# The second part of each weight block: negation on ScalarE and an adding transfer

## The chip, the cores and the metric

The kernel runs on one core of a Trainium2 chip. The metric is the device time of one execution in microseconds, the median of several runs. Inputs lie in HBM, and all weights are read from there once.

## The reference

The program computes two transformer-like blocks over 512 tokens of width 1024 in float32. What matters here is that nearly all its work is matrix products with weights. Cut down:

```
x = x + rmsnorm((sigmoid gates * [ssd_branch(z, xbc, dt), window_attention(q, k, v)]) @ w_o)
x = x + rmsnorm(square(relu(rmsnorm(x) @ w_mlp_in)) @ w_mlp_out)      # 1024 -> 4096 -> 1024
x = x + parallel_mixer(rmsnorm(x))       # mLSTM and latent attention, then w_out
x = x + memory_cross_attention(rmsnorm(x), rmsnorm(mem))
x = x + square(relu(rmsnorm(x) @ w_ff1)) @ w_ff2                      # 1024 -> 4096 -> 1024
```

`z`, `xbc`, `dt`, `q`, `k`, `v` and the gates are columns of one product `rmsnorm(x) @ w_in`. The two MLPs alone hold 64 of the 143 weight blocks described next.

## The kernel before, in words

A float32 product is made of three faster ones. A float32 number is split into a rounded part (type float32r, "hi") and the rest ("lo"), and `hi*xh + hi*xl + lo*xh` stands for `w*x`. So each weight block has to be split before TensorE can use it whole.

The weights come as a stream of 143 blocks, the class `Unit`. Most are 1 MB: 128 partitions, 8 k-tiles, 256 columns. Three tiles belong to a unit: `raw` (as loaded), `whi` and `wlo`, each with two buffers.

- `load()` (line 129) issues the transfer from HBM to `raw` on SyncE's queue (SP).
- `split()` works in two halves of 128 columns. For each half, ScalarE copies `raw` to `whi` with rounding (line 140), and VectorE subtracts, `wlo = raw - whi` (line 141).
- `use(key)` splits the unit if that hasn't been done, and calls `ahead`, which splits the next unit and starts the load of the one after it.

So a unit is split while TensorE works on the unit before it. Its `whi` and `wlo` slots come free when TensorE has read the unit before that one, and a `raw` slot comes free when the readers of the split are done with it.

TensorE's readers come in two kinds. `cm` (channel-major, lines 266 to 268) takes 128 columns of the unit at a time, so its first step needs one half of `wlo` only. `tm` (token-major, lines 284 to 286) takes 128 tokens and all columns, so its first step needs both halves. The woven product `cm4` (lines 1022 to 1024), the query product of the cross-attention (lines 1597 to 1599) and the mixer's projection (lines 1225) and latents read both halves early too.

In the MLPs, `f_evac` works on each 128 columns of the first product: ScalarE makes relu and its rounded square (`ua_h`, lines 1161 and 1162), GpSimd the square `fsq` (line 1164), VectorE the rest `ua_l` (line 1165). The second product is added up in `acc` on VectorE (line 1171). Elsewhere GpSimd adds squares for the norms (line 986), raises to powers (line 323), rotates (line 1279) and issues a few small transfers (lines 561, 626, 1383). A scheduler sets the order on each engine from the program's text. Within an engine the order is then fixed.

Of the kernel before, what the change touches and what calls it, by code (L numbers as in the profile page):

```python
# [43 lines left out]
# columns of w_in  # L44
Z0, XBC0, DT0, Q0, K0, V0, G0 = 0, 2048, 6144, 6208, 7232, 7488, 7744
# columns of w_in_2
U0, VM0, OP0, IF0 = 0, 512, 1024, 1536

# columns of the packed constants
# [3 lines left out]
def packed_constants():  # L53
    """Constants that depend on shapes alone: the identity and its mirror image, the rotary
    frequencies, the one-hot of the relative position buckets, and the fixed rows of the products
    that make the exponents of the decays."""
# [11 lines left out]
    # rows 0..7 choose the chunk, rows 64..127 the pair that a token is in  # L68
# [4 lines left out]
    # rows 8..15 choose the head, rows 64..127 hide the pairs of tokens that a direction doesn't see  # L73
# [11 lines left out]
def body(ctx, tc, a, out, dbg=None):  # L85
# [26 lines left out]
    # ---------------------------------------------------------------- weights, as a stream of blocks  # L112
    win, win2 = a["w_in"][0], a["w_in_2"][0]

    class Unit:
        """A block of weights [128, kt, n], split into two parts of float32r whose sum it is."""
# [14 lines left out]
        def split(self):  # L131
            if self.hi is None:
                self.load()
                self.hi = self.view(wp.tile([P, WN], F32R, name=nm("whi"), tag="whi", bufs=2))
                self.lo = self.view(wp.tile([P, WN], F32R, name=nm("wlo"), tag="wlo", bufs=2))
                n = self.flat or self.n
                for c in range(0, n, max(P, n // 2)):
                    e = min(n, c + max(P, n // 2))
                    sl = (slice(None), slice(c, e)) if self.flat else (slice(None), slice(None), slice(c, e))
                    A.copy(self.hi[sl], self.raw[sl])  # L140
                    V.tensor_tensor(out=self.lo[sl], in0=self.raw[sl], in1=self.hi[sl].bitcast(F32), op=ALU.subtract)  # L141
# [11 lines left out]
    def use(key, lag=False):  # L153
        """The unit; the next one is split at once or, with lag, where ahead() says."""
# [5 lines left out]
    def ahead(key, *behind):  # L160
        """The next unit being split, behind the given instructions, and the one after it on its way."""
# [9 lines left out]
    def evac_first(key, evac, *args):  # L171
        """evac, with the next unit's split behind the first of it on each engine."""
# [78 lines left out]
    # ---------------------------------------------------------------- helpers  # L251
    def cm(key, act, evac, parts=1):
        """Steps of a channel-major product: evac(j, psum) for each 128 columns of the unit, each in
        one step or more."""
# [19 lines left out]
    def tm(key, act, evac, ntile=NT):  # L274
        """Steps of a token-major product: evac(t, psum) for each 128 tokens."""
# [20 lines left out]
    def weave(main, side):  # L296
        """The steps of both lists, each list spread evenly."""
# [13 lines left out]
    def split_from(src, hi, lo, gain=None):  # L311
        """hi + lo = src * gain (a column of gains), both float32r."""
# [7 lines left out]
    def inv_rms(dst, ssq, n, width):  # L320
        """dst = (ssq / n + eps) ** -0.5 for [128, width] columns."""
# [3 lines left out]
    def token_sums(ssq, tag="t"):  # L325
        """Sums over the partitions of [128, 512], token-major in PSUM [128, 4]."""
# [5 lines left out]
    def bcast_tokens(r, tag="t"):  # L332
        """[128, 4] token-major -> PSUM [128, 512] on every partition."""
# [5 lines left out]
    # ---------------------------------------------------------------- persistent tiles  # L339
# [17 lines left out]
    # ---------------------------------------------------------------- block 1, first norm  # L357
# [12 lines left out]
    # the tensor engine's clock is at its full rate when the first inputs are here  # L370
# [34 lines left out]
    # ---------------------------------------------------------------- parameters, as columns  # L405
# [34 lines left out]
    # ---------------------------------------------------------------- dt and the decays  # L440
# [14 lines left out]
    # what the products for the exponents take: see ssd_exponents  # L455
# [4 lines left out]
    def dt_evac(_, po):  # L460
        """Rows (half, direction, head), two chunks of tokens in each half."""
# [17 lines left out]
        # cumulative sums of dt * a in each chunk, forwards and backwards  # L479
# [13 lines left out]
        # cs in two float32r parts, by way of DRAM, where the heads of a group are one row  # L493
# [8 lines left out]
        # the logarithm of dt, less cs, in two parts too  # L502
# [11 lines left out]
        # token-major: exp(cs) and dt * exp(tot - cs)  # L514
# [14 lines left out]
        def late():  # L529
# [8 lines left out]
            # the decay over a whole chunk, on every partition; step k takes chunk k and chunk 3 - k  # L538
# [25 lines left out]
    # ---------------------------------------------------------------- block 1, SSD branch  # L564
# [22 lines left out]
    class Group:  # L587
        """The SSD branch of one group of four heads."""
# [5 lines left out]
        # products, convolution and layouts  # L594
# [27 lines left out]
        # rows of the products for the exponents  # L622
# [32 lines left out]
        def exponents(self, c):  # L655
            """dt[s] exp(cs[l] - cs[s]) of both directions: cs[l] comes from rows 0..7,
            log(dt) - cs[s] from rows 8..15; rows 64..127 hide what overflows on the wrong side, and
            the select what is next to the diagonal."""
# [110 lines left out]
    # ---------------------------------------------------------------- block 1, window attention  # L769
# [8 lines left out]
    # the bias over relative positions, one row for each head, read back as a Hankel block: the  # L778
    # queries of each block are taken in reverse
# [18 lines left out]
    def keys(kv):  # L798
        """The two parts of the keys of a head, each on both halves of the partitions."""
# [11 lines left out]
    def q_steps(u, parts=1):  # L811
        """Queries of a head, in reverse in each block: one part on its own half of the partitions,
        the other part on the other half."""
# [12 lines left out]
    class Pair:  # L826
        """Heads 2 p and 2 p + 1, which have the same keys."""
# [59 lines left out]
        def turn(self, b):  # L887
            """The weights over their sum, transposed, with the queries in order again."""
# [71 lines left out]
    # ---------------------------------------------------------------- residual stream and norms  # L960
# [11 lines left out]
    class SumSq:  # L972
        """Sums of squares over the tiles of a channel-major array."""
# [19 lines left out]
    def post_norm(gain, ssq, next_gain, side):  # L993
        """xT += norm(acc) * gain, and the parts of xT * next_gain; returns the sums of squares of xT.
        The steps of another product run meanwhile."""
# [14 lines left out]
    def cm4(k1, k2, act, evac, lag=3):  # L1010
        """Two units, channel-major, with the parts of the activations taken as they come."""
# [23 lines left out]
    # ---------------------------------------------------------------- block 2, the memory  # L1035
# [25 lines left out]
    # rotary tables with the gains of the norms in them  # L1061
# [84 lines left out]
    def inv_ms_bcast(xsq):  # L1146
        """1 / (mean square + eps) of each token, on every partition."""
# [7 lines left out]
    def mlp(b, xsq, fin, side=(), last=None):  # L1155
        """The tiles of relu(h w1)^2 w2, h without its rms and rb the square of that: fin(m, psum, rb)
        gets the last quarter, the others being in acc, last(m, rb) is called before that."""
# [47 lines left out]
    # ---------------------------------------------------------------- block 2, parallel mixer  # L1205
# [8 lines left out]
    # gates, latents and the shared key: token-major  # L1214
# [42 lines left out]
    # both parts of a head's row are taken by one product  # L1257
# [15 lines left out]
    def rope(dst, src, tabs):  # L1273
        """dst = rotated src [128, 4, 64], the gains being in the tables."""
# [474 lines left out]
```

## Time and profile before

| | |
|---|---|
| median of 3 runs | 1943.59 us (1941.83 to 1944.87) |
| span of the profiled execution | 1939.5 us |
| TensorE (PE) busy | 1868.0 us, 96% |
| VectorE (DVE) busy | 1083.4 us, 56% |
| ScalarE (ACT) busy | 856.8 us, 44% |
| GpSimd (POOL) busy | 482.8 us, 25% |
| DMA, loads from SP (q1) | 157322 packets, 151.03 MB, 24.8% of 16 engines' time |
| DMA, issued by GpSimd (q0) | 2496 packets, 1.61 MB, 0.3% |

The span runs from the first to the last instruction; about 4 us of the measured time lie outside it. The busy table tells which engine has no time left. The windows tell the same for one stage. The timeline of one unit tells how long before its use a split is done, which the sums don't.

### The profile page before, as it was taken

The page shows a single profiled execution, that of the slowest core. Times are in us where ns is not written, and L with a number is a line of the kernel's source. Part 1 is how long each engine was busy: PE and PEld are TensorE (multiplying, and loading weights), DVE is VectorE, ACT ScalarE, POOL GpSimd, SP SyncE. Part 2 cuts the span into 40 slices and gives each one's busy share as a digit, 9 for nine tenths or more (in the row PEclk, how much of TensorE's full clock was granted, in tenths as well). Part 3 has the DMA queues.
Part 4 walks back from the last instruction along what each step waited for, and adds up shares of the span by engine and source line. Part 5 has one row for each costly group of instructions (what it writes and reads, how often), then busy time and mean ns, then how long its engine had stood idle before and what let it go on. Part 6 is the DMA issues. An engine that isn't in the chain of part 4 may idle for free. (4 is left out here: it accounts for less than half of the span.)

```text
span 1939.5 us, 24660 instructions
## 1 busy us (share of the span) xinstructions
PE 1868.0 (96%) x9685; PEld 1541.4 (79%) x9685; DVE 1083.4 (56%) x1751; ACT 856.8 (44%) x1397; POOL 482.8 (25%) x530
## 2 busy tenths in 40 slices
PE   8989999999999999998999999989999999999999
PEld 6878778887887777887888888888877778888887
DVE  7767773777555654537334334667567763334543
ACT  5655652755335665345332323444453543323231
POOL 1544450444202221233011202322110431111020
PEclk9999999999999999999999999999999999999999
DMA  6222122221222221333333332322111213232322
GB/s 174 68 67 67 45 67 87 67 67 44 82 94 82 82 78 66 119 122 109 98 109 98 101 94 89 114 73 74 51 45 65 87 44 108 90 107 87 109 87 65
DMA packets 169377, 164.10 MB, mean 85 GB/s; under 512 B 8742, under 2 KB 165101, under 8 KB 169262
## 3 DMA queue, kind: packets, MB, share of 16 engines
q1 hardware_dynamic: 157322, 151.03, 24.8%
q10 hardware_dynamic: 9444, 9.89, 1.6%
q0 software_dynamic: 2496, 1.61, 0.3%
q8 instruction: 76, 1.25, 0.3%
q14 instruction: 39, 0.32, 0.1%
HBM read 158.26 MB, written 4.23 MB: 84 GB/s over the span
## 5 line engine op out<-in xcount | busy, mean ns | idle before, releaser
L141 DVE TENSOR_TENSOR wlo<-raw,whi 128x1024 fp32r<-128x1024 f32 (+2 forms) x285 | 374.9, 1329 | 277.8 <-ACT whi L140 275.4
L140 ACT CAST whi<-raw 128x1024 fp32r<-128x1024 f32 (+2 forms) x285 | 288.3, 1029 | 408.9 <-PE psg L267 381.1
L266 PE MATMUL psg<-hh,whi 128*128 128x512 f32 (+1 forms) x1016 | 403.0, 397 | 0.8 <-DVE hl L318 0.8
L267 PE MATMUL psg<-hl,whi 128*128 128x512 f32 (+1 forms) x1016 | 400.7, 394 | 0.0
L268 PE MATMUL psg<-hh,wlo 128*128 128x512 f32 (+1 forms) x1016 | 399.3, 393 | 0.0
L266 PE MATMUL psg<-ua_h,whi 128*128 128x512 f32 x800 | 316.5, 396 | 0.5 <-DVE xT L1562 0.5
L267 PE MATMUL psg<-ua_l,whi 128*128 128x512 f32 x800 | 313.4, 392 | 0.0
L268 PE MATMUL psg<-ua_h,wlo 128*128 128x512 f32 x800 | 312.3, 390 | 0.0
L266 PEld LDWEIGHTS psg<-hh,whi 128*128 128x128 f32 (+1 forms) x1016 | 191.0, 188 | 40.5 <-issue 1.2
L268 PEld LDWEIGHTS psg<-hh,wlo 128*128 128x128 f32 (+1 forms) x1016 | 190.7, 188 | 39.7
L267 PEld LDWEIGHTS psg<-hl,whi 128*128 128x128 f32 (+1 forms) x1016 | 190.8, 188 | 38.1 <-DVE hl L315 0.4
L1164 POOL TENSOR_TENSOR fsq<-relu 128x512 f32<-128x512 f32 x64 | 80.9, 1264 | 507.9 <-ACT relu L1161 434.5
L266 PEld LDWEIGHTS psg<-ua_h,whi 128*128 128x128 f32 x800 | 150.1, 188 | 35.4 <-DVE xT L1562 2.4
L267 PEld LDWEIGHTS psg<-ua_l,whi 128*128 128x128 f32 x800 | 150.3, 188 | 32.3 <-DVE ua_l L1165 1.2
L268 PEld LDWEIGHTS psg<-ua_h,wlo 128*128 128x128 f32 x800 | 150.2, 188 | 30.7
L284 PE MATMUL psg<-whi,hh 128*128 128x256 f32 x416 | 121.5, 292 | 2.7 <-ACT sz L608 2.7
L286 PE MATMUL psg<-whi,hl 128*128 128x256 f32 x416 | 121.8, 293 | 0.0
L285 PE MATMUL psg<-wlo,hh 128*128 128x256 f32 x416 | 120.5, 290 | 1.0 <-DVE wlo L141 1.0
L986 POOL TENSOR_TENSOR ssq<-ssq,sq 128x512 f32<-128x512 f32 x42 | 66.4, 1582 | 117.0 <-ACT sq L985 116.0
L1165 DVE TENSOR_TENSOR ua_l<-fsq,ua_h 128x512 fp32r<-128x512 f32 x64 | 47.3, 739 | 79.2 <-POOL fsq L1164 79.2
L284 PEld LDWEIGHTS psg<-whi,hh 128*128 128x128 f32 x416 | 81.5, 196 | 5.9 <-ACT sz L608 4.0
L285 PEld LDWEIGHTS psg<-wlo,hh 128*128 128x128 f32 x416 | 81.4, 196 | 1.6 <-DVE wlo L141 1.2
(560 smaller groups left out, 2910.4 us busy)
## 6 DMA issues: line engine op xcount, KB each, us to landing
raw<-in_w_in_dram SPq DMA_DIRECT2D x37, 1024.0 KB
raw<-in_w_ff_dram SPq DMA_DIRECT2D x32, 1024.0 KB
raw<-in_w_mlp_in_dram SPq DMA_DIRECT2D x16, 1024.0 KB
raw<-in_w_mlp_out_dram SPq DMA_DIRECT2D x16, 1024.0 KB
raw<-in_w_in_dram SPq DMA_DIRECT2D x16, 512.0 KB
raw<-in_w_ssd_out_dram SPq DMA_DIRECT2D x8, 1024.0 KB
raw<-in_w_attn_out_dram SPq DMA_DIRECT2D x4, 1024.0 KB
raw<-in_w_o_dram SPq DMA_DIRECT2D x4, 1024.0 KB
```

The source lines that it names most:

```text
L140: A.copy(self.hi[sl], self.raw[sl])
L141: V.tensor_tensor(out=self.lo[sl], in0=self.raw[sl], in1=self.hi[sl].bitcast(F32), op=ALU.subtract)
L266: T.matmul(o, lhsT=u.hi[:, k, c:e], rhs=xh[k], start=k == 0, stop=False)
L267: T.matmul(o, lhsT=u.hi[:, k, c:e], rhs=xl[k], start=False, stop=False)
L268: T.matmul(o, lhsT=u.lo[:, k, c:e], rhs=xh[k], start=False, stop=k == u.kt - 1)
L284: T.matmul(o, lhsT=xh[k][:, tk], rhs=u.hi[:, k, 0 : u.n], start=k == 0, stop=False)
L285: T.matmul(o, lhsT=xh[k][:, tk], rhs=u.lo[:, k, 0 : u.n], start=False, stop=False)
L286: T.matmul(o, lhsT=xl[k][:, tk], rhs=u.hi[:, k, 0 : u.n], start=False, stop=k == u.kt - 1)
L986: G.tensor_tensor(out=self.t, in0=self.t, in1=q, op=ALU.add)
L1164: G.tensor_tensor(out=f, in0=r, in1=r, op=ALU.mult)
L1165: V.tensor_tensor(out=ua_l[:, m, :], in0=f, in1=ua_h[:, m, :].bitcast(F32), op=ALU.subtract)
```

## The change

For each half of a unit, the subtraction on VectorE goes. In its place ScalarE writes the negative of `raw` into `wlo`, and since `wlo` is of type float32r, what it writes is the negative of the rounded value. Then GpSimd issues a transfer from `raw` to `wlo` within SBUF that adds to what is there: `wlo = -hi + raw`. The rest of the diff removes comments and a docstring, and from line 142 on all lines of the new kernel are one further down.

```
                     A.copy(self.hi[sl], self.raw[sl])
-                    V.tensor_tensor(out=self.lo[sl], in0=self.raw[sl], in1=self.hi[sl].bitcast(F32), op=ALU.subtract)
+                    A.activation(self.lo[sl], self.raw[sl], AF.Copy, scale=-1.0)
+                    nc.gpsimd.dma_start(out=self.lo[sl], in_=self.raw[sl], accum_op=ALU.add)
```

The waits follow: the transfer waits for ScalarE's negation, a reader on TensorE waits for the transfer of its half (`tm` for both), and the next load into the same `raw` slot waits for both transfers. VectorE's list gets 285 instructions shorter, ScalarE's longer by 285 passes and ten table loads, GpSimd's by 285 transfers.

On ScalarE, in the first product of the first MLP (before):

```order
L1161 ACTIVATE relu_9306<-psg_9281 128x512
L1162 ACTIVATE ua_h<-relu_9306 128x512
L140 CAST whi_9343<-raw_9279 128x8x128
L1161 ACTIVATE relu_9337<-psg_9312 128x512
L140 CAST whi_9343<-raw_9279 128x8x128
L1162 ACTIVATE ua_h<-relu_9337 128x512
```

The same place after:

```order
L1162 ACTIVATE relu_9401<-psg_9376 128x512
L1163 ACTIVATE ua_h<-relu_9401 128x512
L140 CAST whi_9438<-raw_9374 128x8x128
L1162 ACTIVATE relu_9432<-psg_9407 128x512
L141 ACTIVATE wlo_9439<-raw_9374 128x8x128
L1163 ACTIVATE ua_h<-relu_9432 128x512
L140 CAST whi_9438<-raw_9374 128x8x128
L141 ACTIVATE wlo_9439<-raw_9374 128x8x128
```

The first negation stands behind the second relu, and the second copy now stands behind the rounded square.

On GpSimd, in the same product (before; `fsq` are the squares of two halves of a unit):

```order
L1164 TENSOR_TENSOR fsq_9239<-relu_9236 128x512
L1164 TENSOR_TENSOR fsq_9270<-relu_9267 128x512
L1164 TENSOR_TENSOR fsq_9309<-relu_9306 128x512
L1164 TENSOR_TENSOR fsq_9340<-relu_9337 128x512
L1164 TENSOR_TENSOR fsq_9379<-relu_9376 128x512
L1164 TENSOR_TENSOR fsq_9410<-relu_9407 128x512
```

The same place after:

```order
L142 DMA wlo_9305<-raw_9250 128x8x128 x2
L142 DMA wlo_9367<-raw_9312 128x8x128 x2
L1165 TENSOR_TENSOR fsq_9404<-relu_9401 128x512
L1165 TENSOR_TENSOR fsq_9435<-relu_9432 128x512
L142 DMA wlo_9439<-raw_9374 128x8x128 x2
L1165 TENSOR_TENSOR fsq_9476<-relu_9473 128x512
```

Both transfers of a unit stand behind two squares. The first two rows are units of the second product before it, where nothing stands between.

On GpSimd in the mixer (before; `lat` and `rs` are powers for norms, `ro` rotations):

```order
L323 TENSOR_TENSOR lat_10207<-lat_10207,mhalf 128x4 x3
L1279 TENSOR_TENSOR ro_10252<-pj_9955,tk_10203 128x128
L1279 TENSOR_TENSOR ro_10256<-pj_9955,tk_10203 128x128
L323 TENSOR_TENSOR rs_1620_10498<-rs_1620_10498,mhalf 128x4 x3
L1279 TENSOR_TENSOR ro_10518<-pj_10405,tq_10205 128x128
L1279 TENSOR_TENSOR ro_10522<-pj_10405,tq_10205 128x128
```

The same place after:

```order
L142 DMA wlo_10470<-raw_10147 128x8x128 x2
L142 DMA wlo_10481<-raw_10477 128x320 x2
L324 TENSOR_TENSOR lat_10392<-lat_10392,mhalf 128x4 x3
L1280 TENSOR_TENSOR ro_10437<-pj_10138,tk_10388 128x128
L1280 TENSOR_TENSOR ro_10441<-pj_10138,tk_10388 128x128
L142 DMA wlo_10621<-raw_10488 128x8x128 x2
L142 DMA wlo_10655<-raw_10628 128x8x128 x2
L324 TENSOR_TENSOR rs_1620_10691<-rs_1620_10691,mhalf 128x4 x3
```

Transfers of four units stand among the powers and rotations, which wait for results of the products.

## Rows read from the trace of the kernel before

**Rows 1.** Page, busy us (share of the span) and number of instructions of each engine:

```profile
PE 1868.0 (96%) x9685; PEld 1541.4 (79%) x9685; DVE 1083.4 (56%) x1751; ACT 856.8 (44%) x1397; POOL 482.8 (25%) x530
```

**Rows 2.** Groups by line and shape: busy us, mean ns | idle before, releasers:

```profile
L141 DVE TENSOR_TENSOR wlo<-raw,whi 128x1024 fp32r<-128x1024 f32 x275 | 368.6, 1354 | 274.5 <-ACT whi L140 274.3
...
L140 ACT CAST whi<-raw 128x1024 fp32r<-128x1024 f32 x275 | 283.6, 1048 | 408.5 <-PE psg L267 381.1 <-issue 11.4 <-PE pse L1226 9.6
...
L665 ACT ACT_TABLE_LOAD x25 | 32.1, 1283 | 0.4
...
L620 ACT ACTIVATE sz<-sz 128x1024 f32<-128x1024 f32 x8 | 8.5, 1060 | 0.0
```

**Rows 3.** First MLP by window: us, busy of PE to POOL, clock, DMA share, GB/s:

```profile
860.00:1205.00 345.00, 339.95 (x1550) 279.78 (x1549) 146.12 (x160) 121.56 (x171) 63.59 (x51) 1.00 0.32 101
```

**Rows 4.** Timeline, one unit of the first MLP: start us, duration us, instruction [idle before]:

```profile
1042.40 2.00 ACT L140 CAST whi<-raw 128x1024 fp32r<-128x1024 f32 x2 [6.24 <-PE psg L267]
...
1043.48 1.22 DVE L141 TENSOR_TENSOR wlo<-raw,whi 128x1024 fp32r<-128x1024 f32 x1 [0.21 <-ACT whi L140]
...
1044.62 1.22 DVE L141 TENSOR_TENSOR wlo<-raw,whi 128x1024 fp32r<-128x1024 f32 x1
...
1045.87 0.37 SPq L129 DMA_DIRECT2D raw<-in_w_mlp_in_dram  x1
...
1053.23 1.05 ACT L140 CAST whi<-raw 128x1024 fp32r<-128x1024 f32 x1 [8.83 <-PE psg L267]
...
1053.71 0.39 PE L268 MATMUL psg<-ua_h,wlo 128*128 128x512 f32 x1
```

**Rows 5.** DMA queue of loads, 132 to 143 us, then 1045.5 to 1056.3: packets, MB, share:

```profile
q1 hardware_dynamic: 2080, 1.05, 35.5%
...
q1 hardware_dynamic: 1040, 1.05, 33.1%
```

**Rows 6.** Small transfers issued by GpSimd: instruction ns min/median/max; after it its landing:

```profile
L626 POOL DMA_DIRECT2D rh<-csd x16: 507/552/641, 42.5 to 424.5; - x16
...
DMA to landing us min/median/max: 1.9/2.0/3.0
...
L1383 POOL DMA_DIRECT2D rows_h<-mk x4: 499/514/648, 1339.6 to 1341.2; - x4
...
DMA to landing us min/median/max: 1.7/1.7/1.9
...
L561 POOL DMA_DIRECT2D rh<-in_consts_dram x2: 540/666/792, 12.2 to 14.1; - x2
```

**Rows 7.** Timeline at the start: unit 1's first copy, and its first product with `wlo`:

```profile
17.77 1.09 ACT L140 CAST whi<-raw 128x1024 fp32r<-128x1024 f32 x1
...
20.75 0.40 PE L268 MATMUL psg<-hh,wlo 128*128 128x512 f32 x1
```

**Rows 8.** Copy and first use of `wlo`, first and last of five units, one half:

```profile
751.55 1.04 ACT L140 CAST whi<-raw 128x1024 fp32r<-128x1024 f32 x1
...
758.46 0.48 PE L268 MATMUL psg<-hh,wlo 128*128 128x512 f32 x1
...
1597.25 1.04 ACT L140 CAST whi<-raw 128x1024 fp32r<-128x1024 f32 x1
...
1603.07 0.39 PE L268 MATMUL psg<-hh,wlo 128*128 128x512 f32 x1
```

**Rows 9.** The same, first and last of eight units that read both halves:

```profile
865.78 1.05 ACT L140 CAST whi<-raw 128x1024 fp32r<-128x1024 f32 x1 [1.07 <-PE psg L267]
...
874.08 0.28 PE L285 MATMUL psg<-wlo,mm_h 128*128 128x256 f32 x1
...
1514.42 1.04 ACT L140 CAST whi<-raw 128x1024 fp32r<-128x1024 f32 x1
...
1519.95 0.39 PE L1599 MATMUL pse<-hh,wlo 128*128 128x512 f32 x1
```

**Rows 10.** Waits of PE: engine line waited for: us in total, times, longest us:

```profile
PE psc L634 <- ACT cT L573: 8.6, 6, 2.3
PE pst L712 <- DVE ua_l L318: 5.8, 4, 2.6
```

## The prediction

> **What bounds the kernel now.** I read four views, in this order. The first is the page's busy table: TensorE works for 1868.0 of 1939.5 us [rows 1], so 71.5 us are idle in all, and no edit that only frees other engines can gain more than a part of them. The second is the table of groups: the line that this change replaces, the subtraction on VectorE, costs 368.6 us of VectorE's time, and the rounding copy ahead of it 283.6 us of ScalarE's [rows 2]. Neither is on the path by its size. The third is the table by windows: in the first MLP TensorE works 339.95 of 345.00 us at a granted clock of 1.00, ScalarE 121.56, GpSimd 63.59, and the DMA engines are at 0.32 of their time [rows 3]. So the stage has room on every engine but TensorE. The fourth is the timeline of one weight unit there [rows 4]: rounding copies from 1042.40, the two subtractions from 1043.48 to 1045.84, the raw slot's next load issued at 1045.87, and the first product with this unit's second part at 1053.71, after a period of 10.83 us (1042.40 to 1053.23). Of 11.31 us from first copy to first use, the old path for the first half uses 2.30 (1.08 to the subtraction, 1.22 of it). That leaves 9.0 us of cover in an ordinary unit. What the change has to be asked is where the cover is thinner than the new path is long.
>
> **The cost of the new path.** Removed: 285 VectorE subtractions. Added: 285 ScalarE passes and 285 adding transfers issued by GpSimd. For one half unit of 128 x 1024:
>
> 1. The copy, 1.05 us [rows 2].
> 2. The negating pass. A ScalarE activation of this size from SBUF to SBUF has a row, 1.06 us [rows 2]. With 0.1 us of hand-over the chain is at 2.2.
> 3. The transfer's fixed part. GpSimd's small transfers land a median of 2.0 us after issue (32 rows) or 1.7 (4 rows), and the issuing instruction takes a median of 0.51, 0.55 and 0.67 us for 4, 32 and 128 rows [rows 6]. I put 2.0 and 0.3 for the step from ScalarE to the issue: 4.5.
> 4. The data. A half is 8 k-tiles of 128 columns in each of 128 partitions, so 1024 pieces of 512 bytes, 64 for each of 16 DMA engines. No row has an adding transfer. Nearest below: a plain load in pieces of 512 bytes, 35.5% of 11 us on 16 engines for 2080 packets, 30 ns a piece. Nearest above: the same engines with pieces of 1 KB, 33.1% of 10.8 us for 1040 packets, 55 ns [rows 5]. An adding piece reads two operands of 512 bytes and writes one, so 1 KB read is what I take it to be like: **55 ns**, 3.5 us for a half. The ends are 30 ns (the second read costs nothing) and 60 (it costs a whole plain piece more).
>
> So the first half is ready 8.0 us after its copy starts. The second half's negation is done at 4.3, its transfer queues behind the first, and both are ready at 11.5. At 30 ns it is 6.4 and 8.5, at 60 ns 8.3 and 12.2.
>
> **Where that is covered.** In a unit of the MLP's second product: 8.0 of 11.31 us. In the first product the order on ScalarE puts a relu (0.6 us) between copy and negation, and on GpSimd both squares ahead of the transfers, so that the first is issued about 3.2 us after the copy and lands at 9.0: still covered, by 2.3. The raw slot comes free at 11.5 instead of 3.4, its load starts 8 us later and has until the second unit from now, 21.7 us after the copy. The DMA engines per period of 10.83 us: 3.57 for the load (33.1% of 10.8) and 2 x 3.5 for the additions, 10.6 in all. That fits, by 2%. The same goes for units of the other stages with periods of 11 to 20 us. I charge nothing there, and a few nanoseconds more a piece would make this the bound (rival B).
>
> **Where it isn't.** I took the time from first copy to first use of the second part for all 143 units. Outside of these it is 9.0 us or more where one half is read first, and 11.0 or more where both are read at once, which leaves at most 0.5 us:
>
> - The start. Unit 1 is copied from 17.77, and its first product with the second part runs at 20.75 [rows 7], 3.0 us later: 8.0 - 3.0 = **5.0**.
> - Five units whose first half is read first, from 751.55 (6.9 us) to 1597.25 (5.8) [rows 8]; the others have 5.8, 6.2 and 5.9. At 8.0 they wait 1.1 + 2.2 + 1.8 + 2.1 + 2.2 = **9.4**.
> - Eight token-major or woven units that read both halves in their first step, from 865.78 (8.3) to 1514.42 (5.5) [rows 9]; between them 6.8, 8.3, 5.8, 7.9, 4.8 and 5.1. At 11.5 they wait 3.2 + 4.7 + 3.2 + 5.7 + 3.6 + 6.7 + 6.4 + 6.0 = **39.5**.
>
> TensorE takes its queue in order, so I count each wait whole. Sum: 53.9 us. By 30 ns a piece: 3.4 + 1.9 + 15.5 = 20.8. By 60: 5.3 + 11.1 + 45.1 = 61.5, and then the MLP's DMA need is 3.57 + 7.68 = 11.25 us, 0.42 over the period in 64 units: 27 more, 88.
>
> The Trainium skill ("DMA: Bandwidth & Descriptors", the anatomy of one DMA on the GpSimd path) fits such transfers as 2.0 us plus bytes over 436 GB/s, which agrees with the 2.0 us landing of [rows 6]. By it a half would need an estimated 1.2 us of data instead of 3.5, under both rows here, and the sum would be about 14 us; [rows 5] shows no engine that moves 512-byte pieces at that pace.
>
> **What the other engines gain and lose.** ScalarE gets 285 x 1.06 = 302 us more, and ten more table loads in its instruction list (1.283 us each [rows 2], 13 us). It goes from 856.8 to about 1170 us, 60%. TensorE now waits for it most at the convolution's silu (line 573), 8.6 us in 6 waits [rows 10]; an ordinary ScalarE pass of 1.06 us ahead of each could add 6 us. VectorE gets 369 us back. TensorE's waits for VectorE are of the kind of `ua_l`, 5.8 us in 4 [rows 10], and each could shorten by up to one subtraction, 1.35 us: 5 us here. Ends: -10 to +15. I take these as cancelling. Before is 1943.6 with 1939.5 profiled, and 4.1 lie outside the span and stay. Forecast: 1943.6 + 53.9 = 1997.5, say **1997**.
>
> **The rivals.**
>
> A is the forecast: waits in thirteen units and the start, 1954 to 2032 by the bounds of one piece's price (20.8 less 10, and 88).
>
> B: the DMA engines become the bound. It decides from 57 ns a piece, where 3.57 + 128 pieces reach 10.83 us. For it: that is 2 ns above what I took, and load and additions have to mix without a gap. Against: 55 is a measured row, and the period may stretch only in 64 of 143 units. At 70 ns: 12.53 us a unit, 1.7 x 64 = 109 in the MLPs, and 76 in the tight units: 2129. At 100 ns: 16.4 us, 354 in the MLPs, about 50 in the other units whose mean period is 15.8, and some 100 in the tight ones: 2448. GpSimd would do the same if writing the pieces took it time by the row: 0.67 us for 128 rows would be 5.3 for 1024, and 10.7 of every 10.83 us. But 4 rows take 0.51 [rows 6], and by the difference 1024 would take 1.8.
>
> The Trainium skill ("Collectives: The Full Stack", Part 3) says of additions made by the DMA that the two source reads halve the rate. That is the 60 ns end, just past B's point.
>
> C: a lock between VectorE and GpSimd. Each transfer is held until VectorE's running operation ends. VectorE's long operations here last 0.7 to 1.35 us, so the chain of 8.0 and 11.5 grows by up to 1.3: 13 units and the start, 18 more, 2015. It lies inside A's span. The Trainium skill ("SBUF — State Buffer", Who interferes with whom) names this trap: GpSimd can't write its transfers' descriptors while VectorE holds the port they share. Here the issues take 499 to 792 ns in [rows 6] with VectorE busy more than half of the time, which shows 0.3 us of it at most.
>
> D: the transfer is hidden (no change). At 8 ns a piece a half has 0.5 us of data, the halves are ready at 5.0 and 7.1, the start and five units still wait, 9.5 us together, and VectorE's relief of up to 10 us gives them back: 1943. It holds from 8 ns downward. Against it: no row moves 512 bytes in under 30 ns.
>
> E, the other side: VectorE's relief decides. VectorE loses 368.6 of its 1083.4 us [rows 1, 2]. If a quarter of TensorE's 71.5 idle us hangs on it, 18 us, and the transfers cost D's 9.5, the result is 1935. It decides where the relief is larger than the new waits. Against it: the same price of a piece, and that by 30 ns the waits alone are 20.8 us.
>
> **How the numbers follow.** A 0.50, with C in it; B up to 2350 0.25; B beyond it (over some 92 ns a piece) 0.10; D 0.08; E 0.07. The predicted time is A's. For 8 in 10 the range takes in A and the nearer part of B: 1946 to 2350. A measurement of this kernel can tell about 0.2%, 3.9 us, from no change. Faster: 0.07. Same: 0.08. Slower: 0.85.
>
> **What would show it.** In the profile after: negations of about 1.06 us on ScalarE; landings of 5.5 us for the first and 9 for the second of two transfers (near 2.5 by D and E, above 7 by B); waits of TensorE for the adding transfer in the units named, 3 to 7 us each, and none in the MLPs; an MLP period that stays at 10.83. A longer period there, with the DMA row of the slices near 9, is B. The forecast is wrong if the price of an adding piece isn't near that of a 1-KB piece, or if the next loads, starting 8 us later, arrive too late in the short units of the mixer.

## The result and the profile after

The changed kernel takes 2143.85 us (median of 4 runs, 2134.34 to 2160.45) against 1943.78. The ratio is 1.104, with a 95% interval of 1.099 to 1.109. The forecast was 1997: the sign was right, the loss of 200 us is almost four times the 54 that were forecast. The time lies in the stated range, near the 2129 of rival B, but the mechanism is not B's.

The page after: busy time, DMA queues, the chain that ended last by engine and then by line, and two groups. The first row answers to [rows 1].

```profile
PE 1932.3 (90%) x9685; PEld 1585.1 (74%) x9685; DVE 738.6 (34%) x1466; ACT 1128.7 (53%) x1692; POOL 874.2 (41%) x815
...
q0 software_dynamic: 281616, 147.68, 59.1%
q1 hardware_dynamic: 157322, 151.03, 22.9%
...
DMA 32%; PE 32%; ACT 11%; POOL 8%; issue 8%; DVE 7%; SPq 1%; ACTq 0%; POOLq 0%; DVEq 0%
...
L142 POOL DMA_DIRECT2D wlo<-raw x285 | 438.5, 1547 | 637.4 <-ACT wlo L141 534.7
...
L141 ACT ACTIVATE wlo<-raw 128x1024 fp32r<-128x1024 f32 (+2 forms) x285 | 295.9, 1038 | 36.2 <-PE psg L286 29.7
```

TensorE has as many instructions as before, but is busy for 64 us longer and idle for 140 us more (211.7 us against 71.5). VectorE was relieved by 345 us, and nothing became faster for it. The windows show where the time went, and that the longer busy time is the clock. Columns are as in [rows 3]; the SSD stage, the first MLP and the mixer, first of before:

```profile
53.30:528.20 474.90, 445.01 (x2513) 378.81 (x2512) 326.63 (x473) 258.62 (x398) 199.01 (x272) 0.98 0.22 66
898.30:1238.50 340.20, 339.41 (x1507) 280.31 (x1506) 132.86 (x142) 109.83 (x148) 56.72 (x48) 1.00 0.32 102
1238.50:1592.20 353.70, 332.61 (x1956) 271.11 (x1955) 247.79 (x510) 167.47 (x317) 87.49 (x87) 1.00 0.21 67
```

The same stages after:

```profile
61.60:558.90 497.30, 451.70 (x2508) 388.09 (x2509) 251.22 (x410) 318.13 (x458) 272.51 (x324) 0.95 0.72 120
962.10:1350.20 388.10, 352.90 (x1507) 284.88 (x1506) 51.44 (x78) 171.55 (x214) 144.55 (x111) 0.97 1.02 171
1350.20:1757.00 406.80, 354.80 (x1953) 291.36 (x1954) 205.42 (x462) 200.09 (x358) 142.02 (x131) 0.92 0.59 111
```

The whole span, cut in every run at the same products with `wlo` (the first ones of units 3, 31, 46 and 89, and the 17th of the woven pairs 57/58 and 111/112), in us, with the difference to before for the profiled execution of each kernel of the experiments below:

| stage | before | after | e1 | e2 | e3 | e4 | e5 | e6 | e8 | e11 |
|---|---|---|---|---|---|---|---|---|---|---|
| start | 53.3 | +8.3 | -2.3 | +5.7 | +7.5 | -2.3 | +14.8 | +0.6 | 0.0 | -0.4 |
| SSD | 474.9 | +22.4 | +26.4 | +14.9 | +19.5 | +1.8 | +32.7 | +21.5 | +3.8 | +17.3 |
| attention | 230.3 | +4.5 | +3.8 | +1.2 | +4.7 | 0.0 | +2.5 | +2.7 | +3.4 | +1.1 |
| output products | 139.8 | +28.7 | +3.0 | +6.5 | +28.8 | -0.2 | +22.6 | +11.9 | +29.7 | +10.7 |
| first MLP | 340.2 | +47.9 | -0.1 | +0.1 | +47.7 | +40.7 | +33.7 | +12.1 | +53.5 | +0.9 |
| mixer and cross-attention | 353.7 | +53.1 | +13.0 | +19.6 | +51.3 | +9.8 | +59.5 | +32.4 | +49.8 | +21.8 |
| second MLP | 347.3 | +39.7 | -0.2 | -0.1 | +12.6 | +52.6 | +27.5 | +15.0 | +46.2 | +1.1 |

The two MLPs, where the forecast charged nothing but 4.4 us for two units, lose 88 of the 205 us. The chain of waits of the changed kernel shows what they wait for. It is given here in order of time, with start, duration and what ran; "issue" is time without a wait that the profile shows:

```profile
1117.54 0.06 ACT whi L140
1117.60 0.89 issue
1118.49 1.06 ACT wlo L141
1119.56 0.35 issue
1119.91 1.55 POOL wlo L142
1121.46 0.33 issue
1121.81 9.10 DMA wlo<-raw
1131.03 10.55 DMA raw<-in_w_mlp_in_dram
1141.64 0.04 issue
1141.68 0.06 ACT whi L140
...
1145.94 9.65 DMA wlo<-raw
1155.72 11.31 DMA raw<-in_w_mlp_in_dram
1167.10 0.04 ACT whi L140
```

The copy itself (1.05 us) is here in the short piece and the "issue" behind it. This is a round: copy and negations, two transfers, and only then the next load into the same raw slot, then the next copy. It takes 24.1 and then 25.4 us; the other slot's round meanwhile takes 22.9 (copies at 1126.90 and 1149.77). There are two raw slots, so a unit takes half of a round on average, 12.1, 12.7 and 11.4 us by these three, and the stage can't go faster. Its units come every 12.31 us on average (28 units from unit 60 to unit 88), 10.98 before. In [rows 4] the same copy waited for TensorE (8.83 us, releaser PE); now a load releases it. The view of ScalarE's waits has 239 us of copies that wait for loads of the MLPs, in 33 waits. The largest kind is the second MLP's (us in total, times, longest); before there is none:

```profile
ACT whi L140 <- DMA raw<-in_w_ff_dram: 124.6, 17, 12.7
```

How long a transfer takes, for all 285 (instruction ns, then issue to landing), answers to [rows 6]:

```profile
L142 POOL DMA_DIRECT2D wlo<-raw x285: 850/1552/2194, 14.4 to 2121.8; - x143
...
DMA to landing us min/median/max: 2.8/8.2/14.8
```

TensorE's waits for the transfers, the two largest kinds, and one for loads of the residual stream `x`, in us in total, times, longest:

```profile
PE psg L269 <- DMA wlo<-raw: 69.4, 35, 4.0
PE psg L286 <- DMA wlo<-raw: 28.2, 10, 8.0
PE pse L1048 <- DMA xk<-in_x_dram: 7.3, 3, 3.0
```

### The profile page after: what moved, and what is told of

It is laid out like the page before. It is cut to its first block, busy times and chain, and to the rows that moved or that the text cites. A ratio compares the mean times of both kernels' runs of the same rounds, so it can differ in the third digit from the quotient of the medians.

```text
span 2144.0 us, 25359 instructions
## 1 busy us (share of the span) xinstructions
PE 1932.3 (90%) x9685; PEld 1585.1 (74%) x9685; DVE 738.6 (34%) x1466; ACT 1128.7 (53%) x1692; POOL 874.2 (41%) x815
## 3 DMA queue, kind: packets, MB, share of 16 engines
q1 hardware_dynamic: 157322, 151.03, 22.9%
## 4 chain that ended last, share of the span: by engine, by line
DMA 32%; PE 32%; ACT 11%; POOL 8%; issue 8%; DVE 7%; SPq 1%; ACTq 0%; POOLq 0%; DVEq 0%
DMA wlo<-raw 17%; DMA raw<-in_w_ff_dram 6%; PE psg L269 5%; PE psg L267 5%; PE psg L268 5%; DMA raw<-in_w_mlp_in_dram 4%; ACT wlo L141 4%; DMA raw<-in_w_mlp_out_dram 3%; POOL wlo L142 2%; ACT whi L140 2%; PE psg L286 2%; PE psg L285 2%; PE psg L287 2%; POOL xd L698 1%; DMA raw<-in_w_in_dram 1%
## 5 line engine op out<-in xcount | busy, mean ns | idle before, releaser
L142 POOL DMA_DIRECT2D wlo<-raw x285 | 438.5, 1547 | 637.4 <-ACT wlo L141 534.7
L269 PE MATMUL psg<-hh,wlo 128*128 128x512 f32 (+1 forms) x1016 | 408.1, 402 | 46.2 <-DMA wlo<-raw 46.2
L267 PE MATMUL psg<-hh,whi 128*128 128x512 f32 (+1 forms) x1016 | 413.0, 406 | 4.4 <-ACT ssq L982 2.2
L268 PE MATMUL psg<-hl,whi 128*128 128x512 f32 (+1 forms) x1016 | 406.6, 400 | 0.0
L141 ACT ACTIVATE wlo<-raw 128x1024 fp32r<-128x1024 f32 (+2 forms) x285 | 295.9, 1038 | 36.2 <-PE psg L286 29.7
L267 PEld LDWEIGHTS psg<-hh,whi 128*128 128x128 f32 (+1 forms) x1016 | 195.6, 192 | 47.5 <-ACT ssq L982 2.6
L286 PE MATMUL psg<-wlo,hh 128*128 128x256 f32 x416 | 126.0, 303 | 17.2 <-DMA wlo<-raw 17.1
L285 PE MATMUL psg<-whi,hh 128*128 128x256 f32 x416 | 127.6, 307 | 3.2 <-ACT sz L609 3.2
L286 PEld LDWEIGHTS psg<-wlo,hh 128*128 128x128 f32 x416 | 86.2, 207 | 20.3 <-issue 20.0
L285 PEld LDWEIGHTS psg<-whi,hh 128*128 128x128 f32 x416 | 86.8, 209 | 5.2 <-ACT sz L609 3.8
```

Of the source, the lines that this page charges most:

```text
L141: A.activation(self.lo[sl], self.raw[sl], AF.Copy, scale=-1.0)
L142: nc.gpsimd.dma_start(out=self.lo[sl], in_=self.raw[sl], accum_op=ALU.add)
L267: T.matmul(o, lhsT=u.hi[:, k, c:e], rhs=xh[k], start=k == 0, stop=False)
L268: T.matmul(o, lhsT=u.hi[:, k, c:e], rhs=xl[k], start=False, stop=False)
L269: T.matmul(o, lhsT=u.lo[:, k, c:e], rhs=xh[k], start=False, stop=k == u.kt - 1)
L285: T.matmul(o, lhsT=xh[k][:, tk], rhs=u.hi[:, k, 0 : u.n], start=k == 0, stop=False)
```

## The experiments

### The parts apart: ScalarE's pass and the transfer

e1 keeps the pass and lets VectorE add.

```
                     A.activation(self.lo[sl], self.raw[sl], AF.Copy, scale=-1.0)
-                    nc.gpsimd.dma_start(out=self.lo[sl], in_=self.raw[sl], accum_op=ALU.add)
+                    V.tensor_tensor(out=self.lo[sl], in0=self.raw[sl], in1=self.lo[sl].bitcast(F32), op=ALU.add)
```

> The negating pass on ScalarE stays, and VectorE adds the raw block to it, so only the transfer goes. If the transfer makes all of the 200 us (theory): 1940 to 1955 us, TensorE's stages as before. If ScalarE's 285 passes of 1.06 us have a share of their own (rival): 1970 us or more, with TensorE waiting for line 141.

Measured: 1982.34 us, ratio 1.0205 (1.0189 to 1.022). The pass alone costs 40 us: the rival's number was right, but its sign (TensorE waiting for line 141) is not seen. 26 of them are in the SSD stage, where ScalarE goes from 258.62 to 322.28 us and TensorE's clock from 0.98 to 0.95 (window, columns as in [rows 3]):

```profile
51.00:552.30 501.30, 456.70 (x2519) 391.26 (x2520) 326.30 (x476) 322.28 (x463) 200.31 (x274) 0.95 0.22 64
```

TensorE's waits there, from 53 to 560 us:

```profile
PE psg L285 <- ACT sz L609: 12.8, 6, 2.5
PE pst L579 <- DVE ua_l L319: 10.3, 6, 2.7
PE pst L713 <- DVE sz L708: 9.2, 11, 2.6
```

The wait for `sz` on ScalarE, a few us before, is now the longest. TensorE has no wait of note for line 142, which makes `wlo` in this kernel. So it is not `wlo` that is late, but other results that ScalarE makes later, and, as far as the lines can tell, those of VectorE that hang on them. In the MLPs, where ScalarE was busy a third of the time before, the pass costs nothing (-0.1 and -0.2).

e2 keeps pass and transfer, and takes the addition away.

```
-                    nc.gpsimd.dma_start(out=self.lo[sl], in_=self.raw[sl], accum_op=ALU.add)
+                    nc.gpsimd.dma_start(out=self.lo[sl], in_=self.raw[sl])
```

> The same transfers without the addition, so wlo is a copy of the raw block and the products are not those of the reference. Theory (the price of an adding piece, 65 to 72 ns, makes the loss): a copied piece takes 27 to 35 ns, the MLPs go back to 340 to 347 us each, the tight units still wait, 1965 to 1990 us in all. Rival (what GpSimd's issue and the transfers' fixed part take, whatever is moved): over 2080 us, with issues still at 1.55 us and MLPs over 375.

Measured: 1993.96 us, ratio 1.0259 (1.0243 to 1.0274). The MLPs are back at their time before, to 0.1 us, as the theory wanted. The total is 4 us over its expected span. ScalarE's pass alone makes 40 us (e1), but the two don't simply nest: in the SSD stage this kernel loses 14.9 us, less than e1's 26.4. GpSimd's queue in the first MLP (1000 to 1200 us; packets, MB, share):

```profile
q0 software_dynamic: 38795, 19.55, 55.4%
```

The view of line 142 gives the issue and the landing of all its transfers:

```profile
L142 POOL DMA_DIRECT2D wlo<-raw x285: 533/878/994, 15.0 to 1962.5; - x143
...
DMA to landing us min/median/max: 2.0/3.9/8.4
```

The same queue in the changed kernel's first MLP (1000 to 1300 us):

```profile
q0 software_dynamic: 51056, 25.74, 75.0%
```

55.4% of 200 us on 16 engines for 38795 packets is 45.7 ns a piece, and 75.0% of 300 us for 51056 is 70.5 ns. A copied piece within SBUF is dearer than the 30 ns load piece of [rows 5] and than the 27 to 35 that were expected, and the addition adds half to it. It brings the landing from 3.9 to 8.2 us.

### The mechanism in the MLPs

e3 adds a third raw buffer from the second MLP on. The first keeps two.

```
+                third = "pool" in extra and pos[self.key] % 3 == 2
-                self.raw = self.view(wp.tile([P, WN], F32, name=nm("raw"), tag="raw", bufs=2))
+                self.raw = self.view((extra["pool"] if third else wp).tile([P, WN], F32, name=nm("raw"), tag="raw3" if third else "raw", bufs=1 if third else 2))
...
     crs.close()
+    extra["pool"] = ctx.enter_context(tc.tile_pool(name="raw3", bufs=1))
```

> As the changed kernel, but from the second MLP on there is a third raw buffer; the first MLP keeps two and is the control in the same run. Theory 1 (the DMA engines' time, 128 pieces of 71 ns and a load of 3.3 us per unit, sets the period): the second MLP stays at 383 to 390 us. Theory 2 (the round of a raw slot sets it: load, copies, negations, two transfers, then the next load, through two buffers): the second MLP falls by more than half of its 40 us, to 350 to 365, and the whole to about 2110 to 2125.

Measured: 2123.71 us, ratio 1.093 (1.0891 to 1.0969). The second MLP falls from 387.0 to 359.9 us, the first stays at 387.9. Per unit: 12.37 us in the first MLP, 11.22 in the second (units 115 to 142), 10.99 before. In its trace no copy of ScalarE waits for a load of the second MLP any more (124.6 us in 17 waits in the changed kernel). Theory 2 holds. The windows of both stages in this one run:

```profile
1000.00:1300.00 300.00, 276.07 (x1175) 221.38 (x1173) 30.88 (x52) 125.71 (x156) 101.80 (x79) 0.98 1.03 174
1800.00:2100.00 300.00, 297.06 (x1306) 241.58 (x1305) 47.06 (x68) 134.75 (x164) 105.91 (x76) 1.00 1.13 183
```

The DMA queues in the same two windows:

```profile
q0 software_dynamic: 50512, 25.46, 73.0%
q1 hardware_dynamic: 25240, 25.45, 28.4%
...
q0 software_dynamic: 55957, 28.21, 84.3%
q1 hardware_dynamic: 27600, 26.48, 28.2%
```

With the same pieces at nearly the same price (69 and 72 ns), the DMA engines moved 10% more packets in the same time as soon as a slot more was there, and their share went from 1.03 to 1.13. A share of 1.03 looked like a full resource and wasn't one. So rival B's reason, that the engines' time sets the period, falls. What is left of the 39.7 us is mostly the entry to the stage: unit 113, one of the five units of [rows 8], waits 4.7 us as it does without the third buffer, and units 114 to 117 another 3.7.

e4 has the new path in the MLPs' units only (`adds` is set where the key begins with `f1` or `f2`).

```
+                    if self.adds:
                         A.activation(self.lo[sl], self.raw[sl], AF.Copy, scale=-1.0)
                         nc.gpsimd.dma_start(out=self.lo[sl], in_=self.raw[sl], accum_op=ALU.add)
+                    else:
+                        V.tensor_tensor(out=self.lo[sl], in0=self.raw[sl], in1=self.hi[sl].bitcast(F32), op=ALU.subtract)
```

> The new path in the 64 units of the two MLPs only, the subtraction everywhere else. If the stages' losses are their own and add up: 1943.6 + 47.9 + 39.7 = 2031 us, 2020 to 2040. If the MLPs only pass on a delay from the units before them, or if part is made good elsewhere: under 2000.

Measured: 2035.59 us, ratio 1.047 (1.0452 to 1.0488). The MLPs' loss is their own: 40.7 and 52.6 us. Of the other stages only the mixer's differs by more than 2.3 us, by 9.8, and its cut takes in the last unit of the first MLP and the first one of the second.

e6 makes the pieces larger: halves of 4 k-tiles of all columns.

```
-                n = self.flat or self.n
-                for c in range(0, n, max(P, n // 2)):
-                    e = min(n, c + max(P, n // 2))
-                    sl = (slice(None), slice(c, e)) if self.flat else (slice(None), slice(None), slice(c, e))
+                n = self.flat or self.kt
+                step = max(P, n // 2) if self.flat else max(1, n // 2)
+                for c in range(0, n, step):
+                    e = min(n, c + step)
+                    sl = (slice(None), slice(c, e))
```

> As the changed kernel, but the halves of a unit are 4 k-tiles of all 256 columns instead of 8 of 128: the same bytes move, in 128 pieces of 4 KB a half instead of 1024 of 512 bytes. Theory (a piece has a fixed price: 53 ns for 288 bytes and 65 to 72 for 512 read as about 38 and 54 per KB, so 260 to 360 ns for 4 KB, and GpSimd's issue falls from 1.55 to under 0.9 us): the round of a raw slot gets some 5 us shorter than 24.6 us and falls below two periods, both MLPs go back to 340 to 350, 1985 to 2020 us in all. Rival (the price goes by bytes, 520 ns or more for 4 KB): MLPs at 375 or more, 2110 us or more.

Measured: 2026.55 us, ratio 1.0431 (1.0384 to 1.0478). The price per byte falls, as expected: the 27.26 MB of the queue in the first MLP are at most 6655 pieces of 4 KB (the rest of its 7486 packets are of 4 bytes), and 49.7% of 290 us for these is some 345 ns a piece, so 43 ns for what 512 bytes cost 70 before. GpSimd's issue falls to 0.87 us, the landing to 5.6 (the view of the line, then the queue from 1000 to 1290 us):

```profile
L143 POOL DMA_DIRECT2D wlo<-raw x286: 831/868/1260, 14.1 to 2010.8; - x143
...
DMA to landing us min/median/max: 2.8/5.6/11.0
```

```profile
q0 software_dynamic: 7486, 27.26, 49.7%
```

The MLPs are at 352.3 and 362.3, over the expected 340 to 350 but most of the way back in the first, and the total is some 7 us over its span. ScalarE's copies still wait 78.6 us for loads of the second MLP (11 times). e13 put the third raw buffer on top of this.

> Halves by k-tiles with pieces of 4 KB, and a third raw buffer from the second MLP on. With two raw buffers and such pieces the second MLP was at 362.3 us. If what was left there is the raw slot's round: 352 us or less. If it is the first use, which with halves by k-tiles needs the second half 2.7 us after the first: 359 to 364 us. First MLP 350 to 354 either way.

Measured: 2022.48 us, ratio 1.037 (1.0313 to 1.0426), with single executions from 1997 to 2039. The profile is of the longest one. In it the second MLP is at 359.9, 11.41 us a unit, the first at 355.8, 11.45 a unit. No copy of ScalarE waits for a load of the second MLP any more, and TensorE's waits for `wlo` there remain, 7.1 us in 10. That points to the first use rather than the round as what is left with large pieces. It isn't shown: no profile tells how long the stage is in the shorter executions, and the total is only 4 us under e6's, whose executions run from 2017 to 2037.

### The SSD stage

e5 lets VectorE make the negation and keeps the transfer.

```
-                    A.activation(self.lo[sl], self.raw[sl], AF.Copy, scale=-1.0)
+                    V.tensor_scalar(out=self.lo[sl], in0=self.raw[sl], scalar1=-1.0, scalar2=None, op0=ALU.mult)
```

> The negating pass is made by VectorE, the adding transfer stays. If ScalarE's pass and the transfer are two losses that add up (40 us and 160 us): 2095 to 2110 us, the SSD stage within 8 us of its 474.9. Rival (VectorE's operations hold up GpSimd's issues, or the loss in the SSD stage is the transfer's too): 2135 us or more, with issues longer than 1.55 us.

Measured: 2141.5 us, ratio 1.1021 (1.0988 to 1.1054), no better than the changed kernel, as the rival had it. The losses of pass and transfer do not add up. The SSD stage loses 32.7 us without ScalarE's pass, and the issues grow:

```profile
L142 POOL DMA_DIRECT2D wlo<-raw x285: 879/1741/3784, 13.1 to 2107.7; - x143
...
DMA to landing us min/median/max: 3.1/9.0/19.2
```

The MLPs, at 373.9 and 374.8 us, gain 12 to 14 us against the changed kernel, 0.4 us a unit; the four kernels with the unchanged path in the first MLP have 380.9 to 393.7 there. That fits the round, though no run isolates it: copy and negation can now run side by side, which takes about 1 us off it.

e8 has the subtraction in the units of the start and the SSD branch, and the new path elsewhere (the condition of e4 with the keys `dt`, `bc`, `x`, `z` and `so` left out).

> The subtraction in the units of the start, the SSD branch and its output product, the new path elsewhere. If stages add up: 2143.9 less 8 at the start and 22 in the SSD stage, 2105 to 2122 us. Rival (the delay there is made good by later stages, which then have less to wait for): 2135 us or more.

Measured: 2125.21 us, ratio 1.093 (1.0899 to 1.0962), 3 us over the expected span. The start is back at 0.0 and the SSD stage at +3.8; the MLPs are 6 us above the changed kernel's. Executions of one kernel differ by more than that (2134 to 2160 us for the changed one), so whether later stages take part of the gain back is not shown.

e11 gives VectorE both passes.

```
-                    A.activation(self.lo[sl], self.raw[sl], AF.Copy, scale=-1.0)
-                    nc.gpsimd.dma_start(out=self.lo[sl], in_=self.raw[sl], accum_op=ALU.add)
+                    V.tensor_scalar(out=self.lo[sl], in0=self.raw[sl], scalar1=-1.0, scalar2=None, op0=ALU.mult)
+                    V.tensor_tensor(out=self.lo[sl], in0=self.raw[sl], in1=self.lo[sl].bitcast(F32), op=ALU.add)
```

> VectorE makes both passes, the negation and the addition, without a transfer and without ScalarE: some 0.65 us a half more for VectorE than before. If the SSD stage waits only for ScalarE and for GpSimd: 475 to 482 us there, 1940 to 1952 in all. If it waits for whichever engine gets more in the order of its queue: 490 us or more there, 1960 or more in all.

Measured: 1994.27 us, ratio 1.0266 (1.0251 to 1.028). The SSD stage loses 17.3 us, the mixer 21.8. That fits stages that wait for whichever of the two engines gets more to do.

e12 puts waiting transfers into GpSimd's queue and leaves everything else.

```
                     V.tensor_tensor(out=self.lo[sl], in0=self.raw[sl], in1=self.hi[sl].bitcast(F32), op=ALU.subtract)
+                    if self.probe:
+                        nc.gpsimd.dma_start(out=wp.tile([P, P], F32R, name=nm("probe"), tag="probe", bufs=2)[0:4, :], in_=self.lo[0:4, 0, c : c + P])
```

> The kernel before with the subtraction, and in the SSD units a transfer of 4 rows of wlo to a scratch tile behind each subtraction, issued by GpSimd and read by nobody. It puts a waiting instruction into GpSimd's queue where the changed kernel has its adding transfers, and moves nothing. If GpSimd's queue held up is what the transfer costs there (theory): SSD stage 485 us or more, 1953 or more in all. Rival (only the late landing of wlo counts): under 479 us, 1941 to 1948 in all.

Measured: 1945.33 us, ratio 1.0013 (1.0003 to 1.0022), the SSD stage +0.8. A short transfer that waits in GpSimd's queue (issued in a median of 0.53 us) costs next to nothing there. The theory that the queue's order alone is the price falls; what an issue of 1.55 us or more costs there is not tested by it.

e10 moves load the other way: of the kernel before, the rounding copy of the second half of the SSD units goes from ScalarE to GpSimd.

```
+                    if self.half and c:
+                        G.tensor_copy(self.hi[sl], self.raw[sl])
+                    else:
                         A.copy(self.hi[sl], self.raw[sl])
```

> The kernel before, with the rounding copy of the second half of each SSD unit moved from ScalarE to GpSimd, so ScalarE is relieved there instead of loaded. If ScalarE's load is what the SSD stage waits for: the stage falls from 474.9 to 460 to 470 us, 1930 to 1940 us in all. Rival (the stage waits for the order of several engines and GpSimd is one of them): 1943 us or more.

Measured: 1952.87 us, ratio 1.0048 (1.0033 to 1.0063), the SSD stage +8.5. Relieving ScalarE at GpSimd's cost is a loss too, although GpSimd's copy takes 1047 ns, as long as ScalarE's.

What stays open: why e5's SSD stage loses 32.7 us. There ScalarE has no pass and VectorE's is shorter than the old subtraction (0.73 us against 1.35), so I take it to be the transfers, by their 1.74 us issues on GpSimd or by VectorE's and GpSimd's operations getting in each other's way. TensorE's largest wait there is for VectorE's `sz` (17.7 us, 4.7 before). No run tells these apart.

### A faster kernel

e7 is the kernel before with e6's halves by k-tiles, so without pass or transfer.

> The kernel before with halves by k-tiles and nothing else. TensorE waits 5 us for wlo in all. Token-major units can start after the first half: 1938 to 1943 us. Rival (channel-major units need the second half 2.7 us after the first, where they had 5.4): 1944 to 1950.

Measured: 1937.31 us, ratio 0.9973 (0.9962 to 0.9984), 0.3% faster than the kernel before and just under the expected span. The mixer's stage is 349.4 us instead of 353.7. Unit 95, a token-major one, is used 1.1 us earlier, where TensorE waited 1.0 us for its `wlo` before: a step of `tm` goes through the k-tiles in order, so it can begin with half of them, where a half of the columns is no use to it. The other 3.3 us are gained in the mixer's projection (units 91 and 92), where TensorE's waits for VectorE's `hl` fall from 5.7 to 3.8 us; why, was not followed. The channel-major units of the MLPs lose nothing (-0.5 and 0.0 us).

## Why the prediction was right or wrong

**The tight units: right in kind, and in the sum partly by luck.** The thirteen units were forecast to wait 48.9 us. Against before they lose 52.8, each counted as the growth of the delay from the unit before it to its own first product. The largest are units 95 (7.7, forecast 6.7), 91 (7.3, 5.7) and 101 (6.5, 6.4); units 93 and 103 lose nothing where 3.6 and 2.1 were forecast. At the price that a piece turned out to have, the prediction's own sum is 76 us with the start (rival B at 70 ns), so misses of both signs cancel. The list was also short by two: units 107 and 112, whose products are woven with a neighbour's, have 2.9 us (copy at 1499.95, first product with `wlo` at 1502.81) and 5.7 us (1580.55, 1586.29), where the text has 9.0 or 11.0 and more for all units outside the list. They lose some 6 us each. The start was forecast at 5.0 and loses 10.7 over its first three units, of which 8.3 are left at unit 3: units 0 and 2 were taken for covered or for one wait with unit 1, and are not.

**The price of a piece: too low.** 55 ns was taken, with 60 as the upper end. The first MLP has 70.5. The lower end was the load's 30 ns, but a copied piece within SBUF takes 45.7, and that row was not to be had before. GpSimd's issue was left inside the 2.0 us landing of 32 rows, where it took 0.55 [rows 6], and takes 1.55 for 1024 pieces. The 0.3 us for the step from ScalarE to it was right (0.35 in the chain). The rows of 4 to 128 pieces did show a rise, and its line through 1024 gave 1.8, which the working named only in a rival and left out of the sum.

**"I charge nothing there": the step that failed.** It stood on two sums. One was the DMA engines' share, 10.6 of 10.83 us. The other was that the raw slot's load, 8 us later, "has until the second unit from now, 21.7 us after the copy". The second sum was never finished: the load's own time was not added. In the chain of waits the load is issued 13.5 us after the copy, not 11.5, and takes 10.6 to 11.3 us beside the transfers of the other unit. That is 24 to 25 us, over 21.7. The MLPs' units pay for it, 79 us without the two that were counted as tight. Another cost that the sum has nothing for is what the transfers do to other loads. Among the output products, unit 53, which had 13.0 us of cover, loses 9.1 us: there TensorE waits for the loads of `x` (7.3 us in 3 waits, see the line above), which in the chain of waits take 5.3 to 7.4 us from issue to landing. Before, it waits for them 0.2 us in all.

**Rival B: a near number for the wrong reason.** Its 2129 us is closest to the result, and its MLPs were to lose 109 us where they lose 88. But e3 shows that the engines were not the bound: with one slot more they moved more. The sign that the prediction named for B, a longer period with the DMA row near 9, is in the profile after (12.31 us, and 9 in most slices of the MLPs). It could not tell B from the slot's round, and e3 does.

**"I take these as cancelling": failed.** ScalarE's pass was bounded at +15 and costs 40 (e1). The bound counted TensorE's present waits for ScalarE and gave each at most one pass. But in the SSD stage new waits arose, among them ones for VectorE (e1); the 13.0 us that e1 loses in the mixer were not followed further. VectorE's relief was to give up to 10 us back. No stage of the changed kernel got faster, so nothing of it can be seen.

**The clock was not in the sum.** A third of the loss, 64 us, is TensorE working more slowly. At unit 95 it waited for 8 us (forecast 6.7, so this is the forecast's own wait). Windows of 8 us around it, columns as in [rows 3]:

```profile
1418.00:1426.00 8.00, 7.57 (x63) 7.15 (x61) 1.53 (x4) 5.71 (x11) 1.62 (x1) 1.00 0.22 37
1426.00:1434.00 8.00, 0.03 (x1) 0.06 (x1) 0.54 (x2) 4.00 (x6) 4.68 (x3) 0.66 1.21 132
1434.00:1442.00 8.00, 8.00 (x49) 8.00 (x50) 1.68 (x4) 1.82 (x4) 0.38 (x1) 0.70 1.15 152
```

After the wait the granted clock is 0.70 over 8 us, so that part of them was at the lower of its two levels (1.2 of 2.4 GHz), and 49 products are made where 63 are made in the window ahead of the wait at 1.00. The wait cost its 8 us and, by these counts, an estimated 2 more. Over the whole run the mean clock went from 0.992 to 0.957, and 1868.0 x 0.992 / 0.957 is 1936, near the 1932.3 us of busy time.

**C and the Trainium skill.** C, a lock between VectorE and GpSimd, is not seen in the changed kernel: issues take 1.55 us in the MLPs, where VectorE has little to do, and as much in the median of the whole run. With VectorE's negation (e5) the median rises to 1.74 and the longest to 3.78, which goes the way that the Trainium skill ("SBUF — State Buffer", Who interferes with whom) says, without showing that a lock is the reason. The fit of the Trainium skill for a transfer ("DMA: Bandwidth & Descriptors", the anatomy of one DMA on the GpSimd path) would give an estimated 3.2 us for 512 KB; e2's plain transfers landed in 3.9, the adding ones in 8.2, and the measurement decides. By the Trainium skill ("Collectives: The Full Stack", Part 3) the two source reads of an addition halve the rate of a copy, in its ring of four ranks; within SBUF the runs here show less, 70.5 against 45.7 ns, 1.5 times.

## What to carry to other kernels

When a step that frees a buffer becomes slower, add up the whole round of that buffer (load, every reader, the next load, each at its time beside the other traffic) and divide it by the number of buffers; compare that with the period before asking whether a resource is full. A full-looking DMA share doesn't prove a bound, and a further buffer is a test. In a stage where several engines feed each other, a pass on an engine that is half idle isn't free, and a long wait of TensorE can cost some more after it, at the lower clock.

## What the runs showed of the hardware that was not expected

- Adding pieces of a transfer within SBUF: 70.5 ns for 512 bytes in the first MLP, against 45.7 ns for a plain copy of the same piece, and some 345 ns for 4 KB (e6). The longer pieces cost about 40% less per byte.
- GpSimd's issue depends on what is issued: 1.55 us for 1024 adding pieces, 0.88 for 1024 plain ones (e2's median), 0.87 for 128 adding ones (e6).
- The DMA share of a window can be over 1.00 (1.13 in e3's second MLP), so the packets' times overlap.
- GpSimd's rounding copy of 128 x 1024 took 1047 ns (e10), the same as ScalarE's 1048 [rows 2].
